# A decoder block on one core: the second FFN's first weights loaded a chunk per gate, the first branch's output and the residual loaded ahead into slots, the mixer's stores on GpSimd's queue

## The chip, the core and the metric

The kernel runs on one core of a Trainium2 chip. The core has TensorE (PE, matrix products into PSUM), VectorE (DVE), ScalarE (ACT), GpSimd (POOL) and SyncE (SP). SP computes nothing here: it issues transfers (DMAs), in the order of its queue, and waits where a transfer's buffer or data isn't ready. GpSimd issues transfers too, also in order, among its few computations. Sixteen DMA engines move the data. The metric is the time of one execution on the device in microseconds (us); lower is better.

## The reference

One layer of a decoder block over 512 tokens of width 1024, all in float32: an FFN, a token mixer and a second FFN, each with its residual, its norm shifted, scaled and gated by vectors computed from a condition `c`.

```python
mod = (silu(c) @ w_ada + b_ada).reshape(3, 3, D)
h = modulate(x, norm_w[0], mod[0,0], mod[0,1]);  x = x + 0.5 * mod[0,2] * swiglu(h, w13[0], w2[0])
h = modulate(x, norm_w[1], mod[1,0], mod[1,1])
proj = h @ w_in                       # latents of the attention, conv_in, gate_logits
o_attn = causal_mla_attention(...)    # 8 heads, blocks of 128 queries
o_conv = gate_b * causal_conv(gate_c * xv)
y_br = [o_attn, o_conv] @ w_branch    # two branches, 512 -> 1024 each
merged = sum(sigmoid(gate_logits) * y_br)
x = x + mod[1,2] * (merged @ w_out)
h = modulate(x, norm_w[2], mod[2,0], mod[2,1]);  x = x + 0.5 * mod[2,2] * swiglu(h, w13[1], w2[1])
```

## The kernel before

All activations lie transposed: eight row tiles (`KD` = 8) of 128 channels by 512 tokens. A float32 product is made of three matmuls (`mm3`, L133): each operand is split into a high part (a cast on ScalarE, L112) and a low part (a subtraction on VectorE, L113), and high x high, high x low and low x high are summed in PSUM. So every weight goes through three steps: a transfer into a raw tile (`raw_load`, L117), the cast, the subtraction.

The mixer has pools of small buffers that are used in turn: `slot` (11 of 128x512), `slot2` (4), `wr` (4 raw weights), `wh` and `wl` (4 high and low halves). Large ones are 17 `block`s. A load into such a buffer waits on its queue until the last user of that buffer is done, and all behind it on the queue wait too.

The order of the mixer around the change is that of the code and of a scheduler which places the instructions on the engines:

- During the attention, the convolution branch and its gates are worked off in between (`under`, L1075). For each row tile `m` of the 8, `gate(1, m, ...)` (L1000) makes a gate product from `w_cg` (8 k-steps, 24 matmuls) and a branch product from `w_br` (4 k-steps, 12 matmuls); the gated result goes out to DRAM (`ycd`, `keep`, L1043), and each head group's attention output to `oad` (L996).
- After the attention, `oad` is read back as `oa` (L1125). Then `gate(0, m, ...)` does the same for the attention branch, and `merge` (L1129) reads `ycd[m]` back into `yc`, adds it, and splits the sum into `mg`, an operand of the output product `wo`. Units of work are run by `stream` (L374): the load of the next unit is issued before the products of this one. After each unit one sum of the condition's vectors (`ada`) is done on VectorE, with its own weight load of 512 KB.
- `out_rows` makes `wo`, 24 matmuls a row tile for the first five; `Residual.put` (L366) forms the new residual from the product and from `xin` (loaded by `fetch`, L359), stores it to `x2d` and feeds the norm `n2`.
- The first weights of the second FFN, eight chunks of 256 KB (`first_raw`, L486, tiles `wfr`), are all issued before the first gate of this stage runs (`wf1`, L1145).

Buffers in the mixer: the gated products, `yc` and `xin` all share the four `slot2`. Queues: everything is on SP's; only the FFNs store on GpSimd's.

Of the kernel before, what the change touches and what calls it, by code (L numbers as in the profile page):

```python
# [13 lines left out]
ALU = mybir.AluOpType  # L14
AX = mybir.AxisListType

P = 128
T = 512
D = 1024
KD = D // P  # L20
# [21 lines left out]
HALF = T // 2  # L42
# [16 lines left out]
def tile_hybrid_block(ctx, tc, xT, pack0, pack1, pos, ada01, ada, w13f0, w13f1, w13a, w13b, w2, w_c, w_cg, w_uq, w_ukv,  # L59
                      w_br, w_out, out):  # L60
    nc = tc.nc
# [8 lines left out]
    def mm(name):  # L70
        return psum.tile([P, T], F32, tag="mm", name=name, bufs=3)

    def aux(name):
        return psum.tile([P, T], F32, tag="aux", name=name, bufs=5)


    def block(name, dt=F32):
        return act.tile([P, 4 * T], dt, tag="block", name=name, bufs=NBLOCK)

    section = {}  # L80
# [9 lines left out]
    def short(tag, n, name, dt=F32):  # L90
        return section["pool"].tile([P, n], dt, tag=tag, name=name, bufs=BUFS[section["kind"]][tag])

    def slot(name, dt=F32):
        return short("slot", T, name, dt)

    def slot2(name, dt=F32):
        return short("slot2", T, name, dt)

    def wide(name, dt=F32):
        return short("wide", WMAX, name, dt)  # L100
# [3 lines left out]
    def halved(t):  # L104
        return t[:, :T], t[:, T:]

    def cols(pair, c0, n):
        return tuple(t[:, c0 : c0 + n] for t in pair)


    def split_to(hi, lo, src):
        nc.scalar.copy(out=hi, in_=src)  # L112
        nc.vector.tensor_tensor(out=lo, in0=src, in1=hi.bitcast(F32), op=ALU.subtract)  # L113
# [6 lines left out]
    def weights(src, n, name):  # L120

        raw = raw_load(src, n, name)
        parts = []
        for c0 in range(0, n, WSUB):
            m = min(WSUB, n - c0)
            hi = short("wh", WSUB, f"wh_{name}_{c0}", F32R)
            lo = short("wl", WSUB, f"wl_{name}_{c0}", F32R)
            split_to(hi[:, :m], lo[:, :m], raw[:, c0 : c0 + m])
            parts.append((hi, lo))
        return lambda i: cols(parts[i * P // WSUB], i * P % WSUB, P)  # L130


    def mm3(ps, a, b, first, last, parts=False):  # L133
        nc.tensor.matmul(ps, a[0], b[0], start=first, stop=False, skip_group_check=parts)  # L134
        nc.tensor.matmul(ps, a[0], b[1], start=False, stop=False, skip_group_check=parts)  # L135
        nc.tensor.matmul(ps, a[1], b[0], start=False, stop=last, skip_group_check=parts)  # L136
# [41 lines left out]
    def mod_col(v, j, n=1):  # L178
        return mod[:, 8 * v + j : 8 * v + j + n]
# [41 lines left out]
    def ada_load(n):  # L221
        for v, k in ada_todo[:n]:
            if section["kind"] == "mixer":
                raw = raw_load(ada[v - 2, k // 2][:, k % 2], D, f"ada_{v}_{k}")
            elif k % 2 == 0:
                pair = block(f"ada_{v}_{k}")
                nc.sync.dma_start(out=pair.rearrange("p (u c) -> p u c", u=2), in_=ada[v - 2, k // 2])
                raw = pair[:, :D]
            else:
                raw = pair[:, D:]  # L230
            ada_ready.append((v, k, raw))
        del ada_todo[:n]
# [16 lines left out]
    def ada_step(n):  # L249
        for _ in range(min(n, len(ada_ready))):  # L250
            ada_unit(*ada_ready.pop(0))
# [98 lines left out]
    class Residual:  # L350
# [8 lines left out]
        def fetch(self, m):  # L359
            if section["kind"] == "ffn":  # L360
                self.xin[m], self.part[m] = halved(wide(f"xin{self.i}_{m}"))
            else:
                self.xin[m] = slot2(f"xin{self.i}_{m}")
            nc.sync.dma_start(out=self.xin[m], in_=self.prev[m])

        def put(self, m, ps, c0=0, n=T):  # L366
            o = self.x[m][:, c0 : c0 + n]
            nc.vector.scalar_tensor_tensor(out=o, in0=ps, scalar=mod_col(self.v, m), in1=self.xin[m][:, c0 : c0 + n],
                                           op0=ALU.mult, op1=ALU.add)
            (nc.gpsimd if section["kind"] == "ffn" else nc.sync).dma_start(out=self.dst[m][:, c0 : c0 + n], in_=o)  # L370

    def stream(units):  # L374
        w = [units[0][0]()]
        yield
        for i, (_, emit) in enumerate(units):
            if i + 1 < len(units):
                w.append(units[i + 1][0]())
            yield from emit(w[i])  # L380

    def whole(name, src, n, rhs, done, spare=False):


        def emit(w):
            ps = mm(f"p_{name}")
            for k in range(n):
                mm3(ps, w(k), rhs[k], k == 0, k == n - 1)
                if k % 4 == 3:
                    if k == n - 1:  # L390
                        done(ps)
                        if spare:
                            if not ada_ready:
                                ada_load(1)
                            ada_step(1)
                            ada_load(min(1, len(ada_todo) - KD))
                    yield

        return (lambda: weights(src, n * P, name), emit)
# [49 lines left out]
    def drain(steps):  # L449
        for _ in steps:  # L450
            pass
# [34 lines left out]
    def first_raw(i, early):  # L486

        n = FIRST[i] * 2 * P
        per = (4 * T if early else WMAX) // n
        for k in range(KD):  # L490
            if k % per == 0:
                t = block(f"wfr{i}_{k}") if early else wide(f"wfr{i}_{k}")
            raw = t[:, k % per * n : (k % per + 1) * n]
            nc.sync.dma_start(out=raw, in_=(w13f0, w13f1)[i][k])
            yield raw
# [308 lines left out]
    n1 = Norm(1, r1.tiles)  # L804
# [71 lines left out]
    oad = dram.tile([4, P, T], F32, name="oad")  # L876
# [66 lines left out]
    class Bank:  # L943
# [38 lines left out]
        def values(self):  # L982
            b, g = self.b, self.g
            if self.h0 == 0:
                po[0] = aux(f"po{b}_{g}")
            for i in range(self.nh):
                h = self.h0 + i
                for kb in range(b + 1):
                    mm3(po[0][:DV, h * P : (h + 1) * P], cols(vb, kb * T + (4 * g + h) * DV, DV),
                        cols(self.pT, (i * (b + 1) + kb) * P, P), kb == 0, kb == b)  # L990
            if self.h0 + self.nh == 4:
                oe = slot(f"oe{b}_{g}")[:, : 2 * P].rearrange("p (c t) -> p c t", c=2)
                for odd in range(2):
                    nc.scalar.copy(out=oe[odd * DV : (odd + 1) * DV],
                                   in_=po[0][:DV].rearrange("p (c o t) -> p c o t", c=2, o=2)[:, :, odd, :])
                nc.sync.dma_start(out=oad[2 * g : 2 * g + 2].rearrange("c p t -> p c t")[:, :, b * P : (b + 1) * P], in_=oe)  # L996

    po = [None]

    def gate(g, m, rhs, done, spare=False):  # L1000

        y = []

        def tanh(pg):
            y.append(slot2(f"gs{g}_{m}"))
            nc.scalar.activation(out=y[0], in_=pg, func=AF.Tanh, scale=0.5)

        def times(py):
            nc.vector.scalar_tensor_tensor(out=y[0], in0=y[0], scalar=1.0, in1=py, op0=ALU.add, op1=ALU.mult)
            done(m, y[0])  # L1010

        return [whole(f"gate{g}_{m}", w_cg[12 + 8 * g + m], KD, n1.h, tanh, spare),
                whole(f"br{g}_{m}", w_br[m][:, 4 * g * P : 4 * (g + 1) * P], 4, rhs, times, spare)]

    oc_b = block("och", F32R), block("ocl", F32R)
    oc = [cols(oc_b, j * T, T) for j in range(4)]
# [24 lines left out]
    ycd = dram.tile([KD, P, T], F32, name="ycd")  # L1041

    def keep(m, y):  # L1043
        nc.sync.dma_start(out=ycd[m], in_=y)

# [74 lines left out]
    oas = [cols(oa_b, j * T, T) for j in range(4)]  # L1122
# [3 lines left out]
        split_to(*oas[j], oa)  # L1126
    mg = [None] * KD

    def merge(m, y):  # L1129
        yc = slot2(f"yc{m}")  # L1130
        nc.sync.dma_start(out=yc, in_=ycd[m])
        nc.vector.tensor_tensor(out=y, in0=y, in1=yc, op=ALU.add)
        if m % 2 == 0:
            mb.append(block(f"mg{m}", F32R))
        z = (m % 2) * 2 * T
        mg[m] = mb[-1][:, z : z + T], mb[-1][:, z + T : z + 2 * T]
        split_to(*mg[m], y)
# [2 lines left out]
    r2 = Residual(2, x1d, 5, x2d)  # L1140
    r2.room()
    n2 = Norm(2, r2.tiles)
    units = [u for m in range(KD) for u in gate(0, m, oas, merge, True)]
    units += out_rows("wo", lambda m: w_out[m], [(0, KD)], mg, r2, n2, (1, 1, 3), True)
    wf1 = list(first_raw(1, True))  # L1145
    wf1 = iter(wf1)
    drain(stream(units))


# [4 lines left out]
            next(n2.steps, None)  # L1154

    r3 = Residual(3, x2d, 8, out)
    ffn(1, n2, ((0, HALF), (HALF, T)), second_chunk, r3, None, (0, 0), wf1)


# [85 lines left out]
```

## Time and profile before

| | us |
|---|---|
| median of the runs shown (3 runs, 1087.56 to 1100.96) | 1089.38 |
| the profiled execution | 1097.2 |
| its span, from the first to the last instruction | 1095.4 |

| share of the span busy | |
|---|---|
| TensorE, matmuls | 95% |
| VectorE | 71% |
| ScalarE | 47% |
| GpSimd | 12% |

In the span the first FFN runs to about 400 us, the mixer to about 750 us (its gates of the attention branch and `wo` from about 627 us), and then the second FFN. The page and the answers of the trace are tables by stretch, lists of waits and instructions in order of time. "SPq" is SP issuing a transfer. PEclk is the granted clock of TensorE as a share of full speed.

### The profile page before, as it was taken

To read this page: it belongs to the slowest core of one execution; us is meant where nothing else is said; L and a number is where in the kernel's file an instruction comes from. 1 tells how busy PE (TensorE), PEld (TensorE's weight loads), DVE (VectorE), ACT (ScalarE), POOL (GpSimd) and SP (SyncE) were. 2 spreads that over 40 slices of the span, in tenths; PEclk is the share of its full clock that TensorE was granted. 3 is DMA by queue.
4 is the path that set the end of the run, shared out by engine and by line. 5 is a ranking of instruction groups with operands and counts; after the bars stand their busy time and mean duration, and the time that the engine had idled before them with its cause. 6 is when DMAs were issued, how large, how long until landed. Compare 5 with 4: busy or idle time off the path is not lost.

```text
span 1095.4 us, 19960 instructions
## 1 busy us (share of the span) xinstructions
PE 1046.0 (95%) x7870; PEld 982.7 (90%) x7870; DVE 782.3 (71%) x1326; ACT 513.9 (47%) x877; POOL 135.7 (12%) x169
## 2 busy tenths in 40 slices
PE   2999989999999989999999989899999999999997
PEld 1999989999999988888887868688999999999997
DVE  6899389855987577767468677648997488834863
ACT  7964345423554154554334433327764255524530
POOL 0001311013100112110000000001101220022001
PEclk9999999999999989999999999899999999999999
DMA  9766987579945423212245486725866894778352
GB/s 367 249 191 197 267 246 206 193 178 272 238 122 205 152 101 97 83 54 68 78 151 187 131 297 235 242 95 155 211 196 223 231 248 128 210 138 216 99 195 85
DMA packets 82254, 198.08 MB, mean 181 GB/s; under 512 B 9584, under 2 KB 12528, under 8 KB 79088
## 3 DMA queue, kind: packets, MB, share of 16 engines
q1 hardware_dynamic: 66256, 164.30, 44.8%
q0 software_dynamic: 15904, 32.51, 15.3%
q8 instruction: 61, 1.00, 0.4%
q14 instruction: 33, 0.27, 0.1%
HBM read 178.95 MB, written 17.83 MB: 180 GB/s over the span
## 4 chain that ended last, share of the span: by engine, by line
PE 76%; DVE 10%; DMA 7%; issue 3%; ACT 1%; SPq 1%; POOL 1%; POOLq 0%; DVEq 0%; ACTq 0%
PE g L134 6%; PE g L135 6%; PE g L136 6%; PE d L135 6%; PE d L136 6%; PE d L134 6%; PE u L134 5%; PE u L135 5%; PE u L136 5%; DMA sa<-in_w13a_dram 2%; DMA wr_ada<-in_ada_dram 2%; DVE ada_acc L199 2%; PE pf L135 1%; PE pf L136 1%; PE pf L134 1%
## 5 line engine op out<-in xcount | busy, mean ns | idle before, releaser
L135 PE MATMUL d<-a,d_h 128*128 128x256 f32 x616 | 171.4, 278 | 1.6 <-DVE a L113 1.6
L136 PE MATMUL d<-a,d_l 128*128 128x256 f32 x616 | 170.9, 278 | 0.0
L134 PE MATMUL d<-a,d_h 128*128 128x256 f32 x616 | 170.9, 278 | 0.0
L134 PE MATMUL u<-T,w_h 128*128 128x256 f32 x456 | 127.8, 280 | 4.0 <-ACT s L567 4.0
L135 PE MATMUL u<-T,w_h 128*128 128x256 f32 x456 | 127.3, 279 | 0.0
L136 PE MATMUL u<-T,w_l 128*128 128x256 f32 x456 | 127.2, 279 | 0.0
L112 ACT CAST w_h<-sa 128x1024 fp32r<-128x1024 f32 x76 | 79.8, 1050 | 81.7 <-issue 48.5
L135 PEld LDWEIGHTS d<-a,d_h 128*128 128x128 f32 x616 | 115.7, 188 | 2.1 <-DVE a L113 2.1
L136 PEld LDWEIGHTS d<-a,d_l 128*128 128x128 f32 x616 | 116.0, 188 | 0.0
L134 PEld LDWEIGHTS d<-a,d_h 128*128 128x128 f32 x616 | 115.9, 188 | 0.0
L113 DVE TENSOR_TENSOR w_l<-sa,w_h 128x1024 fp32r<-128x1024 f32 x76 | 92.5, 1220 | 20.5 <-ACT w_h L112 10.8
L134 PEld LDWEIGHTS u<-T,w_h 128*128 128x128 f32 x456 | 86.2, 189 | 4.9 <-ACT s L567 4.8
L136 PEld LDWEIGHTS u<-T,w_l 128*128 128x128 f32 x456 | 86.7, 190 | 0.0
L135 PEld LDWEIGHTS u<-T,w_h 128*128 128x128 f32 x456 | 86.1, 189 | 0.0
L134 PE MATMUL g<-h,w_h 128*128 128x256 f32 x304 | 84.6, 278 | 0.0
L135 PE MATMUL g<-h,w_h 128*128 128x256 f32 x304 | 84.4, 278 | 0.0
L136 PE MATMUL g<-h,w_l 128*128 128x256 f32 x304 | 84.4, 278 | 0.0
L112 ACT CAST d_h<-wdd 128x1024 fp32r<-128x1024 f32 (+1 forms) x42 | 41.0, 978 | 57.6 <-issue 31.3
L547 DVE TENSOR_TENSOR sb<-sa 128x512 f32<-128x512 f32 x38 | 26.0, 684 | 53.7 <-DMA sa<-in_w13a_dram 32.6
L113 DVE TENSOR_TENSOR d_l<-wdd,d_h 128x1024 fp32r<-128x1024 f32 (+1 forms) x42 | 47.7, 1135 | 16.8 <-ACT d_h L112 11.2
L113 DVE TENSOR_TENSOR w_l<-sb,w_h 128x1024 fp32r<-128x1024 f32 x38 | 46.4, 1220 | 17.5 <-PE g L136 13.5
L136 PEld LDWEIGHTS g<-h,w_l 128*128 128x128 f32 x304 | 57.4, 189 | 0.0
(362 smaller groups left out, 3131.6 us busy)
## 6 DMA issues: line engine op xcount, KB each, us to landing
ada<-in_ada_dram SPq DMA_DIRECT2D x24, 1024.0 KB, 6.7
sa<-in_w13b_dram SPq DMA_DIRECT2D x80, 256.0 KB, 5.0
sa<-in_w13a_dram SPq DMA_DIRECT2D x72, 256.0 KB, 5.3
wdd<-in_w_dram SPq DMA_DIRECT2D x32, 512.0 KB, 4.7
wr_ada<-in_ada_dram SPq DMA_DIRECT2D x24, 512.0 KB, 5.1
sa<-in_w13b_dram POOLq DMA_DIRECT2D x40, 256.0 KB, 6.1
sa<-in_w13a_dram POOLq DMA_DIRECT2D x36, 256.0 KB, 6.3
yd<-yd POOLq DMA_DIRECT2D x32, 256.0 KB, 6.1
```

The lines of the kernel that those rows point to most:

```text
L112: nc.scalar.copy(out=hi, in_=src)
L113: nc.vector.tensor_tensor(out=lo, in0=src, in1=hi.bitcast(F32), op=ALU.subtract)
L134: nc.tensor.matmul(ps, a[0], b[0], start=first, stop=False, skip_group_check=parts)
L135: nc.tensor.matmul(ps, a[0], b[1], start=False, stop=False, skip_group_check=parts)
L136: nc.tensor.matmul(ps, a[1], b[0], start=False, stop=last, skip_group_check=parts)
L199: nc.vector.scalar_tensor_tensor(out=acc, in0=src, scalar=c, in1=acc, op0=ALU.mult, op1=ALU.add)
L547: nc.vector.tensor_tensor(out=b[:, 0], in0=a[:, 3], in1=a[:, 1], op=ALU.add)
```

## The change

- `first_raw` of the second FFN is no longer run through before the stage; each unit that loads branch weights of `gate(0, m, ...)` then calls `ahead(m)`, which loads `ycd[m]` into a `slot` and issues the next chunk of `wfr`.
- `merge` adds the tile that was loaded there and issues no load.
- `xin` of the mixer's residual is a `slot` instead of a `slot2`.
- The stores to `oad`, `ycd` and `x2d` are issued by GpSimd instead of SP.

```diff
@@ Residual.fetch, Residual.put
-                self.xin[m] = slot2(f"xin{self.i}_{m}")
+                self.xin[m] = slot(f"xin{self.i}_{m}")
...
-            (nc.gpsimd if section["kind"] == "ffn" else nc.sync).dma_start(out=self.dst[m][:, c0 : c0 + n], in_=o)
+            nc.gpsimd.dma_start(out=self.dst[m][:, c0 : c0 + n], in_=o)
@@ Bank.values
-                nc.sync.dma_start(out=oad[2 * g : 2 * g + 2].rearrange("c p t -> p c t")[:, :, b * P : (b + 1) * P], in_=oe)
+                nc.gpsimd.dma_start(out=oad[2 * g : 2 * g + 2].rearrange("c p t -> p c t")[:, :, b * P : (b + 1) * P], in_=oe)
@@ gate
-    def gate(g, m, rhs, done, spare=False):
+    def gate(g, m, rhs, done, spare=False, ahead=lambda m: None):
...
-        return [whole(f"gate{g}_{m}", w_cg[12 + 8 * g + m], KD, n1.h, tanh, spare),
-                whole(f"br{g}_{m}", w_br[m][:, 4 * g * P : 4 * (g + 1) * P], 4, rhs, times, spare)]
+        load, emit = whole(f"br{g}_{m}", w_br[m][:, 4 * g * P : 4 * (g + 1) * P], 4, rhs, times, spare)
+
+        def load_ahead():
+            w = load()
+            ahead(m)
+            return w
+
+        return [whole(f"gate{g}_{m}", w_cg[12 + 8 * g + m], KD, n1.h, tanh, spare), (load_ahead, emit)]
@@ keep
-        nc.sync.dma_start(out=ycd[m], in_=y)
+        nc.gpsimd.dma_start(out=ycd[m], in_=y)
@@ merge and the stage's units
+    yc = {}
+
+    def ahead(m):
+        yc[m] = slot(f"yc{m}")
+        nc.sync.dma_start(out=yc[m], in_=ycd[m])
+        wf1.append(next(wf1_loads))
+
     def merge(m, y):
-        yc = slot2(f"yc{m}")
-        nc.sync.dma_start(out=yc, in_=ycd[m])
-        nc.vector.tensor_tensor(out=y, in0=y, in1=yc, op=ALU.add)
+        nc.vector.tensor_tensor(out=y, in0=y, in1=yc[m], op=ALU.add)
...
-    units = [u for m in range(KD) for u in gate(0, m, oas, merge, True)]
+
+    wf1, wf1_loads = [], first_raw(1, True)
+    units = [u for m in range(KD) for u in gate(0, m, oas, merge, True, ahead)]
     units += out_rows("wo", lambda m: w_out[m], [(0, KD)], mg, r2, n2, (1, 1, 3), True)
-    wf1 = list(first_raw(1, True))
-    wf1 = iter(wf1)
     drain(stream(units))
...
-    ffn(1, n2, ((0, HALF), (HALF, T)), second_chunk, r3, None, (0, 0), wf1)
+    ffn(1, n2, ((0, HALF), (HALF, T)), second_chunk, r3, None, (0, 0), iter(wf1))
```

The order of the transfers is where the change is seen. On SP's queue at the start of the attention branch's gates stood, from the read-back `oa` to the branch weights of gate 2 (numbers behind names are the program's buffers):

```order
L1125 DMA oa_7155<-oad 128x512
L1125 DMA oa_7159<-oad 128x512
L494 DMA wfr_0_7165<-in_w13f_dram 128x512 x4
L494 DMA wfr_4_7170<-in_w13f_dram 128x512 x4
L1131 DMA yc_7248<-ycd 128x512
L117 DMA wr_ada_3_7293<-in_ada_dram 128x1024
L117 DMA wr_gate_2_7295<-in_w_cg_dram 128x1024
L1131 DMA yc_7319<-ycd 128x512
L117 DMA wr_ada_4_7326<-in_ada_dram 128x1024
L117 DMA wr_br_2_7328<-in_w_br_dram 128x512
```

and in the changed kernel, at the same place:

```order
L1131 DMA oa_7155<-oad 128x512
L1131 DMA oa_7159<-oad 128x512
L1139 DMA yc_7181<-ycd 128x512
L494 DMA wfr_0_7183<-in_w13f_dram 128x512
L1139 DMA yc_7256<-ycd 128x512
L494 DMA wfr_0_7183<-in_w13f_dram 128x512
L117 DMA wr_ada_3_7288<-in_ada_dram 128x1024
L117 DMA wr_gate_2_7290<-in_w_cg_dram 128x1024
L117 DMA wr_ada_4_7319<-in_ada_dram 128x1024
L117 DMA wr_br_2_7321<-in_w_br_dram 128x512
L1139 DMA yc_7327<-ycd 128x512
L494 DMA wfr_0_7183<-in_w13f_dram 128x512
```

Two chunks of `wfr` now stand ahead of gate 2's weights instead of eight; the others follow, one behind each `yc`.

At the end of the gates SP's queue had, from gate 7's branch weights to the load of the last `yc`:

```order
L117 DMA wr_br_7_7697<-in_w_br_dram 128x512
L117 DMA wr_ada_7_7732<-in_ada_dram 128x1024
L117 DMA wr_wo_0_0_7736<-in_w_out_dram 128x1024
L117 DMA wr_wo_0_0_7784<-in_w_out_dram 128x1024
L1131 DMA yc_7687<-ycd 128x512
L117 DMA wr_wo_0_0_7827<-in_w_out_dram 128x1024
L117 DMA wr_wo_0_0_7869<-in_w_out_dram 128x1024
L117 DMA wr_wo_0_0_7911<-in_w_out_dram 128x1024
L364 DMA xin_0_7734<-x1d 128x512
L1131 DMA yc_7760<-ycd 128x512
```

and has now:

```order
L117 DMA wr_br_7_7696<-in_w_br_dram 128x512
L1139 DMA yc_7702<-ycd 128x512
L494 DMA wfr_4_7486<-in_w13f_dram 128x512
L117 DMA wr_ada_7_7734<-in_ada_dram 128x1024
L364 DMA xin_0_7736<-x1d 128x512
L117 DMA wr_wo_0_0_7738<-in_w_out_dram 128x1024
L364 DMA xin_1_7782<-x1d 128x512
L117 DMA wr_wo_0_0_7784<-in_w_out_dram 128x1024
L117 DMA wr_wo_0_0_7827<-in_w_out_dram 128x1024
```

The last `yc` stood behind five loads of `wo` weights and now stands behind gate 7's branch weights, ahead of all of them. On GpSimd's queue, which had nothing between the attention's powers and the norm's, stand now the stores; these are its rows from the last of the attention to the second FFN:

```order
L996 DMA oad<-oe_0_6942 128x2x128
L1050 DMA ycd<-gs_7_7034 128x512
L996 DMA oad<-oe_1_7141 128x2x128
L370 DMA x2d<-x_0_7163 128x512 x4
L370 DMA x2d<-x_1_7164 128x512
L370 DMA x2d<-x_1_7164 128x256 x3
L287 TENSOR_TENSOR nr_0_8098<-nv_0_8096,mhalf 128x2
L370 DMA x2d<-x_1_7164 128x256 x3
L287 TENSOR_TENSOR nr_2_8275<-nv_2_8273,mhalf 128x2
L537 DMA sa_2_8469<-in_w13b_dram 128x512
```

The computations on GpSimd keep their order; the stores are put between them. On TensorE the order of the matmuls is the same but for a few around the first two branch k-steps.

## Rows read from the trace of the kernel before

**Rows 1.** Page, part 1: busy us (share of the span) xinstructions.

```profile
PE 1046.0 (95%) x7870; PEld 982.7 (90%) x7870; DVE 782.3 (71%) x1326; ACT 513.9 (47%) x877; POOL 135.7 (12%) x169
```

**Rows 2.** By stretches: length; busy PE, PEld, DVE, ACT, POOL; PEclk, DMA share, GB/s.

```profile
630.00:640.00 10.00, 9.43 (x40) 6.97 (x38) 5.16 (x9) 2.57 (x5) 0.00 (x0) 1.00 1.01 378
670.00:680.00 10.00, 10.00 (x44) 8.03 (x43) 6.90 (x12) 2.87 (x5) 0.00 (x0) 1.00 0.79 277
700.00:710.00 10.00, 6.33 (x15) 4.67 (x16) 5.84 (x10) 3.33 (x5) 0.00 (x0) 0.66 0.60 179
900.00:1000.00 100.00, 100.00 (x884) 100.00 (x884) 61.98 (x83) 46.35 (x65) 14.76 (x18) 1.00 0.66 155
```

**Rows 3.** Waits of TensorE, 440 to 780 us: total us, times, longest.

```profile
PE wo L134 <- ACT mg L112: 3.4, 1, 3.4
PE p_gate L134 <- ACT wh_gate L112: 2.6, 1, 2.6
...
PE wo L135 <- DVE mg L113: 0.4, 1, 0.4
PE p_br L134 <- ACT oah L112: 0.3, 1, 0.3
```

**Rows 4.** TensorE in order of time: start, us, form [idle before <- releaser].

```profile
642.30 0.50 PE L134 MATMUL p_gate<-h,wh_gate 128*128 128x512 f32 x1 [2.58 <-ACT wh_gate L112]
...
677.21 0.39 PE L134 MATMUL p_gate<-h,wh_gate 128*128 128x512 f32 x1
...
699.55 0.40 PE L136 MATMUL wo<-mg,wl_wo 128*128 128x512 f32 x1
703.32 0.79 PE L134 MATMUL wo<-mg,wh_wo 128*128 128x512 f32 x1 [3.37 <-ACT mg L112]
...
709.33 0.50 PE L134 MATMUL wo<-mg,wh_wo 128*128 128x512 f32 x1
```

**Rows 5.** ScalarE in order of time, the same columns.

```profile
630.14 0.62 ACT L112 CAST oah<-oa 128x512 fp32r<-128x512 f32 x1
...
641.63 1.14 ACT L112 CAST wh_gate<-wr_gate 128x512 fp32r<-128x512 f32 x2 [2.56 <-DMA wr_gate<-in_w_cg_dram]
```

**Rows 6.** SP's queue in order of time: start, us, transfers issued.

```profile
624.40 0.37 SPq L996 DMA_DIRECT2D oad<-oe  x1
...
626.71 0.94 SPq L1125 DMA_DIRECT2D oa<-oad  x2
627.70 4.13 SPq L494 DMA_DIRECT2D wfr<-in_w13f_dram  x8
...
633.69 0.33 SPq L117 DMA_DIRECT2D wr_gate<-in_w_cg_dram  x1
...
689.37 6.27 SPq L117 DMA_DIRECT2D wr_wo<-in_w_out_dram  x3
...
696.16 0.42 SPq L1131 DMA_DIRECT2D yc<-ycd  x1
```

**Rows 7.** VectorE in order of time, columns as in rows 4.

```profile
676.52 0.69 DVE L113 TENSOR_TENSOR wl_gate<-wr_gate,wh_gate 128x512 fp32r<-128x512 f32 x1 [1.34 <-ACT wh_gate L112]
...
692.61 0.69 DVE L1132 TENSOR_TENSOR gs<-gs,yc 128x512 f32<-128x512 f32 x1 [0.60 <-DMA yc<-ycd]
...
695.80 0.68 DVE L1009 SCALAR_TENSOR_TENSOR gs<-gs,p_br 128x512 f32<-128x512 f32 x1
...
701.92 0.69 DVE L1132 TENSOR_TENSOR gs<-gs,yc 128x512 f32<-128x512 f32 x1 [4.84 <-DMA yc<-ycd]
...
703.73 0.68 DVE L113 TENSOR_TENSOR mg<-gs,mg 128x512 fp32r<-128x512 f32 x1
```

**Rows 8.** Tiles `x1d`, `x2d`: issues (ns min/median/max), landing of `x1d`, of `x2d` (also loads).

```profile
L370 POOL DMA_DIRECT2D x1d<-x x12: 539/540/584, 351.6 to 391.6; - x12
...
DMA to landing us min/median/max: 2.0/2.8/5.9
DMA to landing us min/median/max: 1.7/2.6/4.9
```

## The prediction

> **What bounds the kernel now.** I read the page first: TensorE is busy 95% of the span [rows 1], so only the stretches in which it is not busy, or runs slowly, can give time back. The table by stretches places them for the stage that is changed: 900 to 1000 us, the second FFN, has TensorE busy for all 100 us, while 700 to 710 us has 6.33 us of 10 and a granted clock of 0.66 [rows 2]. Then the list of waits of TensorE from 440 to 780 us, mixer and start of the second FFN: the two largest are 3.4 us for an operand of the output product `wo` (a cast to `mg`), plus 0.4 us for its low part, and 2.6 us for gate weights [rows 3]. They are what the change can reach, as the next three views show.
>
> The first stall ends at 642.30 us: a matmul of gate 2 waits 2.58 us [rows 4]. What it waits for is the cast of the gate's weights on ScalarE at 641.63 us, and that stood idle 2.56 us for the transfer [rows 5]. The transfer was issued at 633.69 us, behind eight `wfr` loads that take SP's queue from 627.70 us for 4.13 us [rows 6]. They are 8 x 256 KB = 2.1 MB, and with all else 630 to 640 us moved 378 GB/s at a DMA share of 1.01 [rows 2]: 2.1 MB at that rate are 5.5 us. So this stall is the eight loads' doing.
>
> The second stall ends at 703.32 us, after 3.37 us [rows 4], and the low part adds 0.4 us [rows 3]. It is row tile 7 of the merged branches. VectorE has its gated product at 695.80 us, then stands 4.84 us until `yc` lands and adds it at 701.92 us; the low part follows at 703.73 us [rows 7]. That `yc` load was issued only at 696.16 us, behind three `wr_wo` loads which hold SP's queue from 689.37 us for 6.27 us [rows 6]. What it reads was stored by the stage before, so it is late only by its place in the queue and its wait for a `slot2`.
>
> This stall has a second price. From 699.55 us (the last matmul before it) to 709.33 us (the first that comes at the old pace again) there are 13 steps [rows 4]. The matmuls around it start every 0.233 us; those between start every 0.427 us, in the stretch whose granted clock is 0.66 [rows 2]: the lower of the two levels, 1.2 instead of 2.4 GHz. 13 steps at 0.233 us are 3.03 us; they took 9.78 us. The stall thus costs 6.75 us: some 3.75 us of waiting and 3 us of slow clock. The first stall has no such tail.
>
> **The change, part by part.**
>
> *First weights a chunk per gate.* The same eight loads, the same bytes, now one behind each `yc` load. Ahead of gate 2's weights stand two instead of eight: 1.5 MB fewer, at 378 GB/s 4.2 us, and six issues fewer, of 4.13/8 = 0.52 us each. The gate's transfer would be issued near 631 us and land near 636 to 638 us, where it was 641.6 us; TensorE wants it at 642.30 - 2.58 = 639.72 us. Gain 2.58 us. Ahead of it on VectorE now stand two sums of `ada` and one low part, about 0.7 us each, which end before 640 us if the transfers land by 637.5 us. If the bandwidth is what 670 to 680 us shows, 277 GB/s [rows 2], they land a little later and half a microsecond comes back; I count that below.
>
> The six other chunks go into the gates 2 to 7. There the weights have one raw buffer per gate, so each load waits until VectorE has split the one before, and the slack is small: for gate 6 the first low half is done at 676.52 + 0.69 = 677.21 us [rows 7] and TensorE starts at 677.21 us, needing it from its third matmul on, 0.47 us later [rows 4]. If TensorE comes 2.58 us earlier, the weights must as well. They start earlier by about as much, since the whole ring hangs on gate 2's split. But a chunk of 256 KB takes 0.9 us at 277 GB/s, and it stands ahead of the `ada` and gate loads of its turn. Lower bound nothing (the queue is idle for microseconds between a branch's load and the next), upper bound 0.9 us in each of six gates, 5.4 us. I take 0.5 us: one late gate, since the bound is reached only if nothing of the chunk moves in the idle time, and the DMA share in 670 to 680 us is 0.79.
>
> *The first branch's output loaded ahead.* Same eight loads, each now issued right behind the branch weights of its own gate. Those weights must be there before the branch product starts, 12 matmuls or 2.8 us before the product is done, and `yc` lands soon after them: no wait for it is left. After the change the add comes as soon as VectorE has done the product and the reduction that stands between (0.6 us each); from the start of the add to the end of the low part the rows have 703.73 - 701.92 + 0.68 = 2.49 us. So the low part is ready near 695.80 + 0.6 + 0.6 + 2.5 = 699.5 us, counted on the old times. Also gone is the wait of the tile before it, 0.60 us on the same engine [rows 7]. TensorE would ask for it at 699.78 us at the earliest. That is close, but everything ahead of it shifts with the first stall. Gain 6.75 us, lower bound 3 us (a wait of 1 us left and some slow clock), upper bound 6.75 us.
>
> *The residual in slots.* `xin` leaves the four `slot2` buffers for eleven slots. No wait of TensorE after 709 us names it, so nothing is gained; its cover is the 5.6 us that each row of `wo` takes. Loads 2 to 7 now stand behind `wr_wo` loads; VectorE needs load 2 only after three rows of products. Nothing, unless that cover is gone, and then as late as the load.
>
> *Stores on GpSimd's queue.* Twenty-seven stores leave SP's queue: eight `oad`, eight `ycd`, eleven `x2d`. SP waited for their data, but the list names no wait of TensorE for weights before gate 2's, so nothing is gained there. GpSimd issues one in 0.54 us (`x1d` in the first FFN, twelve of the shapes of `x2d`) [rows 8]. What queues behind them there is the norm's power (`nr`), wanted microseconds after the last store, and that of the attention; both keep their cover. One store is on the path: the last `oad`, issued at 624.40 us, is read back by two loads at 626.71 us [rows 6], and their cast at 630.14 us [rows 5] makes TensorE wait 0.3 us already [rows 3]. From GpSimd the store takes 0.2 us more to issue (0.54 against 0.37 us), and landing goes by the medians 2.8 against 2.6 us for stores of `x` on the two queues; the worst are 5.9 and 4.9 us [rows 8]. So 0.4 us lost, bounds 0 and 3.5 us (5.9 against the 2.3 us that this one took).
>
> The Trainium skill (SBUF — State Buffer, section "SBUF: two separate sides") says that a DMA issued from GpSimd has its descriptors written by that engine, which VectorE locks out while it runs in certain modes; it gives 620 ns alone against 3100 ns beside such a copy. By it the last store would be 2.5 us late and the gain smaller by as much. The rows of `x1d`, 539 to 584 ns beside a busy VectorE, don't show it.
>
> **Sum.** 2.58 + 6.75 - 0.5 - 0.4 = 8.4 us. The profiled execution took 1097.2 us, so it would take 1088.8 us; it lies 7.8 us above the median of the runs shown, 1089.4 us. If the stalls are the same there, the median becomes **1081.0 us**. The second FFN is bound by TensorE, so it starts and ends earlier by all of it.
>
> **The rivals.**
>
> *The gate ring gives the first stall back.* For it: the 0.47 us of slack and a DMA share that rises from 0.79 to about 0.9 (0.9 us of transfer in the 36 matmuls or 8.4 us of a gate). Against: the ring starts earlier too. Only the second stall is gained, with the store's 0.4 us and up to 2 us more lost: 1089.4 - 6.35 = 1083.0 us, up to 1085 us.
>
> *The store is late on GpSimd.* 2.5 to 3.5 us at the first branch product instead of 0.4 us: 1083.1 to 1084.1 us. A lock by VectorE would do it (the page above); the rows speak against it.
>
> *The operand stays late.* The last `mg` waits for its turn on VectorE behind splits of `wo` weights that themselves land late. Half or all of the 6.75 us stays: 1084.4 to 1087.7 us. For it: the weights' transfers and the add share one engine in order. Against: the product was there at 695.80 us.
>
> *Slower: the chunks starve the ring.* `yc` and chunk, 512 KB a gate, stand ahead of `ada` and gate weights, 1.8 us at 277 GB/s; six gates late by that are 10.9 us, and one stall as long as the second brings the slow clock, 3.0 us more. Against the gain of 9.3 us this is a loss of 4.6 us: 1094 us. It decides from 1.55 us of delay per gate on. Against: the bytes are the same in all and far fewer before 640 us, and a transfer that stands ahead of another costs it nothing when it goes out microseconds earlier.
>
> **Chances.** Forecast 0.62, the ring gives back 0.13, store late 0.08, operand late 0.10, slower 0.07. 1076 to 1090 us: below it 1080 less the scatter of some 3 us about the lowest of the runs shown; above it the slower case. About 2% is what a measurement of this kernel can tell from no change; that is 22 us, and all stalls within reach add up to 9.6 us. So faster by over 2% 0.01, within 2% 0.97, slower by over 2% 0.02 (the ring late by 4 us a gate).
>
> **What would show it.** Gate 2 without a wait, and 630 to 640 us with a DMA share under 0.9: the first step. No wait of `wo` for `mg`, and a granted clock of 1.00 through the stretch of `wo`: the second. The wait of the first branch product for `oah` of 0.5 to 0.9 us: the store. A new wait at gates 5 or 6 is the ring. It is wrong if TensorE's idle time in 600 to 710 us doesn't fall, or if the second FFN takes longer.

## The result and the profile after

The changed kernel takes 1084.42 us (median of 20 runs, 1082.0 to 1096.28) where the kernel before, timed beside it, takes 1093.12 us (20 runs, 1086.19 to 1105.61). The ratio is 0.9933, 95% interval [0.9912, 0.9955]: 7.3 us less, between 4.9 and 9.6. That is no change by the 2% bound, and a small gain that the interval keeps away from 1. The profiled execution took 1083.25 us, its span 1081.4 us.

Page of the changed kernel, part 1, to set beside [rows 1]: busy us (share) xinstructions.

```profile
PE 1037.5 (96%) x7870; PEld 976.3 (90%) x7870; DVE 782.1 (72%) x1326; ACT 514.2 (48%) x877; POOL 151.9 (14%) x196
```

The work is the same; GpSimd alone has more of it, 196 instructions instead of 169, which are the 27 stores. The waits of TensorE from 440 to 780 us, as in [rows 3], now name neither `wh_gate` nor `mg`:

```profile
PE pf L136 <- DVE wfl L113: 1.2, 2, 0.7
...
PE p_br L134 <- ACT oah L112: 0.4, 1, 0.4
```

Stretches of the changed kernel, columns as in [rows 2]:

```profile
630.00:640.00 10.00, 10.00 (x45) 8.05 (x44) 8.78 (x14) 3.26 (x6) 0.00 (x0) 1.00 0.97 347
700.00:710.00 10.00, 10.00 (x44) 8.02 (x43) 4.48 (x7) 2.66 (x5) 1.08 (x2) 1.00 0.56 212
900.00:1000.00 100.00, 100.00 (x885) 100.00 (x884) 60.10 (x80) 45.71 (x64) 18.25 (x21) 1.00 0.72 179
```

700 to 710 us had TensorE busy for 6.33 us at a granted clock of 0.66; now it is busy throughout at 1.00, and 630 to 640 us too. The second FFN runs as before (885 matmuls in 100 us against 884).

The next two views give the reasons. SP's queue of the changed kernel, columns as in [rows 6]:

```profile
624.50 0.36 SPq L1139 DMA_DIRECT2D yc<-ycd  x1
624.90 0.43 SPq L494 DMA_DIRECT2D wfr<-in_w13f_dram  x1
...
626.86 0.38 SPq L117 DMA_DIRECT2D wr_gate<-in_w_cg_dram  x1
...
672.20 0.42 SPq L1139 DMA_DIRECT2D yc<-ycd  x1
```

and its VectorE, columns as in [rows 7]:

```profile
687.92 0.68 DVE L1009 SCALAR_TENSOR_TENSOR gs<-gs,p_br 128x512 f32<-128x512 f32 x1
...
689.12 0.69 DVE L1143 TENSOR_TENSOR gs<-gs,yc 128x512 f32<-128x512 f32 x1
...
690.91 0.69 DVE L113 TENSOR_TENSOR mg<-gs,mg 128x512 fp32r<-128x512 f32 x1
```

Gate 2's weights are issued at 626.86 us behind two chunks (before: 633.69 us, behind eight [rows 6]). The last `yc` is issued at 672.20 us, 15.7 us ahead of the product it is added to (before: 696.16 us, behind that product [rows 6, 7]). Its add has no idle time ahead of it, and the last low part of `mg` starts 2.99 us after its product instead of 7.93 us.

**The yardstick.** Executions of one and the same kernel lie up to 20 us apart (last section), so the variants below are told apart by two parts of the stage, read from TensorE's timeline of each profile: from the first product of the attention branch (`p_br<-oah`) to the first of `wo`, which holds the first stall, and from there to the first sum of the norm behind `wo` (`ps_ss`), which holds the second. The three matmuls in before:

```profile
627.69 0.39 PE L134 MATMUL p_br<-oah,wh_br 128*128 128x512 f32 x1
...
694.80 0.48 PE L134 MATMUL wo<-mg,wh_wo 128*128 128x512 f32 x1
...
740.10 0.58 PE L282 MATMUL ps_ss<-ones_c,nacc 128*128 128x1 f32 x4
```

and in after:

```profile
624.31 0.39 PE L134 MATMUL p_br<-oah,wh_br 128*128 128x512 f32 x1
...
688.23 0.48 PE L134 MATMUL wo<-mg,wh_wo 128*128 128x512 f32 x1
...
726.68 0.58 PE L282 MATMUL ps_ss<-ones_c,nacc 128*128 128x1 f32 x4
```

| kernel | branch to `wo`, us | `wo` to norm sum, us | both |
|---|---|---|---|
| before | 67.11 | 45.30 | 112.41 |
| after | 63.92 | 38.45 | 102.37 |
| after once more (e11) | 64.28 | 38.45 | 102.73 |

The stage is 10.0 us shorter. The spans of the profiled pair differ by 14.0 us; of the rest, 3.4 us lie ahead of the stage (it starts at 627.7 and at 624.3 us, and over all kernels here anywhere from 622.5 to 627.7 us, whatever the edit), and 0.6 us behind it.

### The profile page after: what moved, and what is told of

Its sections match the earlier page's. It is cut to its first block, busy times and chain, and to the rows that moved or that the text cites. A ratio compares the mean times of both kernels' runs of the same rounds, so it can differ in the third digit from the quotient of the medians.

```text
span 1081.4 us, 19989 instructions
## 1 busy us (share of the span) xinstructions
PE 1037.5 (96%) x7870; PEld 976.3 (90%) x7870; DVE 782.1 (72%) x1326; ACT 514.2 (48%) x877; POOL 151.9 (14%) x196
## 4 chain that ended last, share of the span: by engine, by line
PE 58%; issue 14%; DVE 3%; POOL 2%; DMA 1%; ACT 1%; POOLq 0%; DVEq 0%; ACTq 0%; SPq 0%
PE d L135 5%; PE d L136 5%; PE d L134 5%; PE g L134 4%; PE g L135 4%; PE g L136 4%; PE u L134 3%; PE u L135 3%; PE u L136 3%; PE p_gate L136 2%; PE p_gate L134 2%; PE p_gate L135 2%; PE wo L134 1%; PE wo L135 1%; PE wo L136 1%
## 5 line engine op out<-in xcount | busy, mean ns | idle before, releaser
L134 PEld LDWEIGHTS g<-h,w_h 128*128 128x128 f32 x304 | 57.2, 188 | 0.2 <-ACT s L572 0.2
```

## The experiments

**One part undone at a time.** First the chunks, all eight up front again (e1):

```diff
-    wf1, wf1_loads = [], first_raw(1, True)
-        wf1.append(next(wf1_loads))      # in ahead(m)
+    wf1 = list(first_raw(1, True))       # before the units run
```

> The changed kernel, but the eight chunks of the second FFN's first weights are all issued ahead of the stage again. Theory A (each stall has its own cause, the chunks the first): TensorE waits 2 to 3 us for gate 2's weights, no wait for the last mg; from the first gate of the stage to wo 73.5 us instead of the changed kernel's 70.5 us, from wo to the second half's norm sum 38.5 us as in the changed kernel; 3 us above the changed kernel. Rival B (the loads ahead and the stores, not the chunks, free gate 2): no wait at gate 2, the changed kernel's time.

Measured: 69.47 and 38.45 us; time 1096.18 us, ratio to before 0.9967 [0.9929, 1.0005]. The first stall is back, alone and larger: waits of TensorE from 440 to 780 us in this kernel,

```profile
PE p_gate L134 <- ACT wh_gate L112: 3.7, 1, 3.7
```

and its stretches (columns as in [rows 2]):

```profile
640.00:650.00 10.00, 7.80 (x26) 5.93 (x27) 7.63 (x12) 3.10 (x6) 0.00 (x0) 0.83 0.74 232
...
850.00:900.00 50.00, 50.00 (x427) 50.00 (x426) 30.14 (x42) 19.46 (x28) 12.68 (x17) 1.00 0.89 238
```

Two loads of `yc` now stand ahead of gate 2's weights, where before had one, which fits a wait of 3.73 us instead of 2.58 us; and here it is followed by half speed: granted clock 0.83, seven steps of about 0.427 us between matmuls. The price is 69.47 - 63.92 = 5.6 us. Theory A has the cause right, and both of its sizes (2 to 3 us of wait, 3 us in all) are too small. The chunks per gate are what removes the first stall, and with `yc` loaded ahead they are worth 5.6 us instead of the 67.11 - 63.67 = 3.4 us that they bring alone (e4 below). The row of 850 to 900 us is taken up in the last section.

Then `yc` in the merge again, from a `slot2` (e2):

```diff
-        yc[m] = slot(f"yc{m}")                     # in ahead(m)
-        nc.sync.dma_start(out=yc[m], in_=ycd[m])
+        yc = slot2(f"yc{m}")                       # in merge
+        nc.sync.dma_start(out=yc, in_=ycd[m])
```

> The changed kernel, but yc is loaded in merge from slot2 again, the chunks stay one per gate. Theory A: no wait at gate 2; the wait of wo for the last mg is back, 3 to 4 us, and with it a granted clock near 0.66 in the ten us after, so 45 us instead of 38.5 us from wo to the norm sum; 6 to 7 us above the changed kernel. Rival B (xin in its own slots is what frees the last yc, since xin and yc no longer share slot2): no wait, the changed kernel's time.

Measured: 64.75 and 39.21 us; 1095.67 us, ratio 0.9973 [0.9935, 1.0011]. The second stall does not come back; of the waits for `mg` only this one is left:

```profile
PE wo L135 <- DVE mg L113: 0.5, 1, 0.5
```

This was the miss that mattered: with `yc` late in the code, and still in a `slot2`, it lands in time but for 0.5 us. So something else of the change must also remove the second stall.

Then the three stores on SP's queue again (e3):

```diff
-            nc.gpsimd.dma_start(out=self.dst[m][:, c0 : c0 + n], in_=o)   # so also oad, ycd
+            (nc.gpsimd if section["kind"] == "ffn" else nc.sync).dma_start(out=self.dst[m][:, c0 : c0 + n], in_=o)
```

> The changed kernel, but the stores to oad, ycd and x2d stay on SP's queue. Theory A (the stores cost and bring nothing): the changed kernel's time within 1 us, the wait for oah 0.3 instead of 0.4 us, no wait at gate 2 or at the last mg. Rival B (the stores hold SP's queue and so the loads behind them): waits of TensorE for gate weights or for mg of more than 1 us, 2 to 6 us above the changed kernel.

Measured: 63.89 and 38.46 us, as in after to 0.03 us; 1093.44 us, ratio 0.9962 [0.9925, 0.9999]. Between these two kernels the stores neither gain nor cost anything that the stage shows: the wait for `oah` is 0.25 us here and 0.40 us in after, and the part is no shorter. Two other pairs of kernels are set beside this one further down.

**One part alone.** The kernel before with the chunks per gate and nothing else (e4):

> The kernel before, with only the chunks of first weights spread, one per gate. Theory A: the wait at gate 2 is gone, the wait for the last mg stays at 3 to 4 us with its slow clock: 3 us under the kernel before. Rival B (the ring of gate weights gives the gain back): waits of 2 us or more at gates 5 to 7, the time of the kernel before.

Measured: 63.67 and 44.54 us; 1097.52 us, ratio 1.0008 [0.9976, 1.0039]. The first stall is gone, the second is whole (waits of TensorE, 440 to 780 us):

```profile
PE wo L134 <- ACT mg L112: 3.4, 1, 3.4
...
PE wo L135 <- DVE mg L113: 0.7, 1, 0.7
```

What holds the last `yc` stands in the chain of waits of the kernel before, which the prediction did not read (start, us, what the chain passes through):

```profile
686.81 0.61 DVE wl_gate L113
...
687.44 0.33 SPq L117
...
687.82 4.69 DMA yc<-ycd
...
692.61 0.70 DVE gs L1132
...
694.59 0.69 DVE wl_wo L113
...
695.31 0.33 SPq L117
...
695.68 0.42 SPq L364
...
696.16 5.66 DMA yc<-ycd
```

Read from the top: a gate's low half frees a raw buffer, only then SP can issue a `wr_wo` (L117), and `yc` 6 goes out behind it and lands at 692.5 us. VectorE, in order, adds it at 692.61 us and so comes to the split of a `wo` weight only at 694.59 us; that frees the raw buffer for the next `wr_wo` at 695.31 us; behind it on SP's queue stands `xin` 0 (L364), and behind that `yc` 7. One late load makes the next one late, through VectorE and the raw buffers, and `xin` 0 is a link, though by itself it holds the queue only from 695.68 to 696.16 us, 0.48 us. `yc` 7 does not wait for its `slot2`: it goes out as soon as `xin` 0 is issued.

The next run (e5) tests that: the kernel before, with the chunks per gate and the residual in slots; `yc` and stores as before.

```diff
-                self.xin[m] = slot2(f"xin{self.i}_{m}")
+                self.xin[m] = slot(f"xin{self.i}_{m}")
```

> The kernel with yc late, but the stores on SP's queue: chunks per gate and xin in slots are all that is left of the change. Theory A (the slots of xin are what lets the last yc go out earlier, since xin 0 no longer stands between): at most 1 us of waits for the last mg, granted clock 1.00 through wo, 38.5 to 39.5 us from wo to the norm sum. Rival B (the stores on SP held it): a wait of 3 us or more for mg, some 45 us.

Measured: 64.02 and 38.69 us, 1084.01 us in a single execution (before, a single one: 1101.61 us). Both stalls are gone without `yc` ahead. It differs from e4 in the residual's buffers alone, and the second part falls from 44.54 to 38.69 us (39.74 in e10, the same kernel): with the chunks per gate, the residual in slots is enough. SP's queue of this kernel:

```profile
679.01 0.33 SPq L117 DMA_DIRECT2D wr_wo<-in_w_out_dram  x1
679.40 0.41 SPq L1140 DMA_DIRECT2D yc<-ycd  x1
679.91 6.86 SPq L117 DMA_DIRECT2D wr_wo<-in_w_out_dram  x4
686.83 0.43 SPq L1140 DMA_DIRECT2D yc<-ycd  x1
```

`yc` 6 stands behind one `wr_wo`, and no `xin` stands ahead of `yc` 7: that one goes out 2.03 us before the first matmul of `wo` (688.86 us), where before it went out 1.36 us after it (696.16 against 694.80 us). The 0.48 us of `xin` 0 are a small part of that. The order of the queue has changed too: in before and e4 two `wr_wo` loads stand ahead of `yc` 6. What it does is seen in VectorE's add of `yc` 6, in e4

```profile
689.32 0.69 DVE L1141 TENSOR_TENSOR gs<-gs,yc 128x512 f32<-128x512 f32 x1 [0.92 <-DMA yc<-ycd]
```

and in e5:

```profile
683.76 0.68 DVE L1141 TENSOR_TENSOR gs<-gs,yc 128x512 f32<-128x512 f32 x1
```

In e4 VectorE still waits 0.92 us for `yc` 6 (0.60 us in before [rows 7]), in e5 not at all: there the chain no longer runs through `yc` 6.

The kernel before with only `yc` loaded ahead (e6):

> The kernel before with yc loaded ahead into slots, and nothing else: chunks up front, xin in slot2, stores on SP. Theory A (each stall has its own cause): 2.5 to 4 us of wait at gate 2, none for mg, 38.5 us from wo to the norm sum. Rival B (the second stall is a late consequence of the first, through the ring of gate weights): the wait for mg stays at 1 us or more.

Measured: 70.07 and 38.45 us; 1089.04 us in a single execution. The second stall is gone, with `xin` left in `slot2`. The first has grown as in e1 (3.22 us, granted clock 0.96 and 0.87 in 630 to 650 us); the part costs 70.07 - 67.11 = 3.0 us more than before. And with only the stores on GpSimd (e7):

> The kernel before with the stores to oad, ycd and x2d on GpSimd's queue, and nothing else. Theory A: both stalls stay, 2.5 us or more at gate 2 and 3 us or more for mg with the slow clock, about 67 us to wo and 45 us on to the norm sum. Rival B (without stores on SP's queue the loads of gate 2 and of the last yc go out in time): one of the two waits falls under 1 us.

Measured: 67.71 and 44.61 us; 1095.33 us in a single execution. Both stalls stay: 3.0 us at gate 2, 2.5 and 0.4 us at `wo`, granted clock 0.66 in 700 to 710 us.

**The residual alone, and the two edits timed.** Timed side by side: before with only `xin` in slots (e9), the kernel of e5 again (e10), and the changed kernel again (e11).

> The kernel before with one edit: the residual `xin` in the eleven slots instead of the four `slot2` buffers; the eight `wfr` loads stay up front, `yc` stays in the merge and in `slot2`, the stores stay on SP's queue. Theory A (a chain: the second stall needs `xin` 0 ahead of `yc` 7 on SP's queue and in `slot2`): this alone removes it, wait of `wo` for `mg` at most 1 us, 38.4 to 39.5 us from the first matmul of `wo` to the first norm sum (44.5 to 45.3 with the stall, 38.45 without), gate 2's wait stays at 2.5 to 3.7 us, 67 to 68 us from the first branch product to `wo`. Theory B (the prediction's step: `xin` brings nothing, `yc` is late by its own place behind the `wr_wo` loads): the wait of 3 us or more stays, 44 to 46 us. Theory C (the chunks per gate are needed too, since in the run of chunks and `xin` slots both were there): 41 us or more, and the wait between 1 and 3 us.

Measured: 68.31 and 41.01 us; 1095.97 us, ratio 0.9986 [0.9941, 1.0031]. Its waits of TensorE, 440 to 780 us:

```profile
PE p_gate L134 <- ACT wh_gate L112: 2.1, 1, 2.1
PE wo L134 <- ACT mg L112: 1.4, 1, 1.4
...
PE wo L135 <- DVE mg L113: 0.7, 1, 0.7
PE p_gate L136 <- DVE wl_gate L113: 0.6, 1, 0.6
```

Neither theory A (38.4 to 39.5 us) nor B (44 to 46 us) holds by its numbers; theory C does, at its edge (41 us or more, 1 to 3 us of wait). This edit takes 45.30 - 41.01 = 4.3 of the 6.85 us: the slow clock (granted clock 1.00 in 700 to 710 us) and 1.7 us of the wait. The rest needs the chunks per gate or `yc` ahead. What in the chunks brings it was not tried; SP's queue shows only that `yc` 6 stands here behind two `wr_wo` loads, as in before, where in e5 it stood behind one:

```profile
681.90 0.93 SPq L117 DMA_DIRECT2D wr_wo<-in_w_out_dram  x2
682.88 0.42 SPq L1131 DMA_DIRECT2D yc<-ycd  x1
684.43 6.25 SPq L117 DMA_DIRECT2D wr_wo<-in_w_out_dram  x3
690.74 0.43 SPq L1131 DMA_DIRECT2D yc<-ycd  x1
```

VectorE waits 0.60 us for `yc` 6 here as in before, so the chain is still there, only earlier. Against the first matmul of `wo`, `yc` 7 goes out 1.46 us sooner than in before: 0.48 us are `xin` 0, the other 1.0 us the `wr_wo` load ahead of it. Why that load is sooner is not shown. The stall at gate 2 costs 68.31 - 67.11 = 1.2 us more here, and loads that do not wait for TensorE may have got ahead by it; so the 4.3 us are not for certain the residual's alone. The comparison of e4 and e5 has no such doubt, since neither has a stall at gate 2.

> The kernel before with the chunks one per gate and `xin` in slots, no more; seen once before with 64.02 and 38.69 us in the stage's two parts (after: 63.92 and 38.45). Theory A: these two edits are the whole gain, so its time and that of the changed kernel in this same call differ by less than 0.3%, and its ratio to the kernel before is 0.990 to 0.997. Theory B: the loads of `yc` ahead or the stores on GpSimd bring something that the stage's two parts don't show: then it is slower than the changed kernel by 0.3% or more.

Measured: 64.18 and 39.74 us (0.65 us of wait for a low part of `mg`); 1091.22 us, ratio 0.9957 [0.9911, 1.0003].

> The changed kernel once more, on the chip of this call. By the stage: 63.9 us from the first branch product to `wo` and 38.5 us to the first norm sum, 10 us less than the kernel before, whatever the pace of the FFNs. By the time: a ratio of 0.990 to 0.995 if the stage is all there is; 0.996 or more if the FFNs give part of it back.

Measured: 64.28 and 38.45 us; 1086.07 us, ratio 0.9917 [0.9869, 0.9966], before 1094.22 us. By the stage the two kernels differ by 1.2 us, by the medians by 5.15 us, 0.5%. Both kernels' times fall into two groups with 5.5 us or more between them (e10: five runs from 1083.74 to 1087.55 and five from 1094.90 to 1098.84; e11: eight from 1080.53 to 1089.83 and two above 1095), so the medians depend on how many fell into each, and ten runs don't settle it. By the medians theory A fails (under 0.3%) and theory B's 0.3% is reached, but the scatter is larger than either. Whether `yc` ahead is worth more than the stage's 0.3 to 1.2 us over these two edits stays open.

**The second stall over all kernels.** The issue of the last `yc` against the first matmul of `wo`, from the two timelines:

| kernel | last `yc` issued, us from the first `wo` matmul | waits of `wo` for `mg`, us | `wo` to norm sum, us |
|---|---|---|---|
| e4, chunks only | +1.65 | 3.4 + 0.7 | 44.54 |
| before | +1.36 | 3.4 + 0.4 | 45.30 |
| e7, stores only | +1.14 | 2.5 + 0.4 | 44.61 |
| e9, `xin` only | -0.10 | 1.4 + 0.7 | 41.01 |
| e10, chunks and `xin` | -0.44 | 0.65 | 39.74 |
| e2, all but `yc` ahead | -1.12 | 0.5 | 39.21 |
| e5, chunks and `xin` | -2.03 | none | 38.69 |
| after | -16.03 | none | 38.45 |

The three at the top lie within 0.8 us and are not in order; below them the part gets shorter the sooner `yc` goes out. Of the kernels not listed, e1, e3, e6 and e11 have it out 17 to 33 us ahead and take 38.45 or 38.46 us, and e8 (below) has it out 13 us ahead, its 39.44 us holding a wait for a `wo` weight. With `yc` out 1.12 us ahead 0.5 us of wait was left, with 2.03 us none; the change has it out 16 us ahead.

**The ring loaded harder.** The rival "slower" said that more bytes ahead of the gates' weights starve them. The changed kernel with 512 KB more per gate (e8), in two loads into slots that nothing reads:

```diff
         wf1.append(next(wf1_loads))
+        for z in range(2):
+            nc.sync.dma_start(out=slot(f"more{m}_{z}"), in_=ycd[m])
```

> The changed kernel with 512 KB more per gate: two more loads of 256 KB behind each chunk, into slots that nobody reads. Theory A (the ring of gate weights has some slack; a chunk of 256 KB fits, three times as much does not): waits of 0.5 to 2 us at several of the gates 3 to 7, in all 3 to 8 us more from the first branch product to wo. Rival B (the queue's idle time takes them): no wait at a gate, 64 us to wo as in the changed kernel. Rival C of the prediction (the chunks already fill the ring): 10 us or more.

Measured: 68.20 and 39.44 us; 1092.40 us in a single execution. Its waits of TensorE, 440 to 780 us:

```profile
PE p_gate L136 <- DVE wl_gate L113: 2.2, 2, 1.2
...
PE p_gate L134 <- ACT wh_gate L112: 0.8, 1, 0.8
PE wo L136 <- DVE wl_wo L113: 0.7, 1, 0.7
```

768 KB a gate instead of 256 KB cost 68.20 - 63.92 = 4.3 us, with waits at gates 2 and 6 (theory A had the sum, not the gates): the rival's mechanism exists at three times the chunk. What lies between was not tried. How much of it is bandwidth (630 to 640 us: 387 GB/s) and how much the waits for two more slots, this run does not part.

## Why the prediction was right, step by step

The forecast was a gain of 8.4 us and no change by 2%. Measured are 7.3 us [4.9, 9.6] and, timed a second time, 1094.22 x 0.0083 = 9.1 us [3.7, 14.3] by the ratios, and 10.0 and 9.7 us in the stage of the profiles. Right in class and near in size; not every step was right. That 8.4 lies so near 7.3 us is partly luck: for the stage the sum is 1.6 us short (3.2 + 6.85 = 10.0 us against 8.4), by 0.6 us of the first stall, 0.1 of the second, 0.5 of the ring and 0.4 of the stores.

- **First stall, 2.58 us.** Right in its cause: e1 and e4 show that the eight chunks made it and the chunks per gate remove it. The size was too small: the part fell by 67.11 - 63.92 = 3.2 us. The prediction took the listed wait alone and wrote that this stall has no tail. It has a short one, in before:

```profile
639.32 0.40 PE L136 MATMUL p_br<-oah,wl_br 128*128 128x512 f32 x1
...
643.44 0.40 PE L134 MATMUL p_gate<-h,wh_gate 128*128 128x512 f32 x1
```

  Between these two lie four steps; they took 4.12 us, where four at 0.233 us are 0.93 us: 3.19 us.
- **The ring, 0.5 us lost.** No loss is seen: no gate waits, and the kernels with chunks per gate (after, e2 to e5, e10, e11) lie between 63.67 and 64.75 us. e8 shows how far the limit is.
- **Second stall, 6.75 us.** The size was right, half speed included: 45.30 - 38.45 = 6.85 us. The timing too: low part ready 690.91 + 0.69 - 687.92 = 3.7 us after the start of the product, predicted 699.5 - 695.8 = 3.7 us.
- **"Late only by its place in the queue and its wait for a `slot2`"; "the residual in slots: nothing is gained".** This is the step that failed. In e2 `yc` keeps its place in the code, behind five `wr_wo` loads, and its `slot2`, and comes in time; between e4 and e5 the residual alone is worth 4.8 to 5.9 us, between before and e9 4.3 us. The stall was held by a chain over SP's queue, VectorE and the raw buffers, which more than one edit breaks. The prediction saw the `wr_wo` loads ahead of `yc` 7 but not what the last of them waited for, and it asked only whether TensorE waits for `xin`, not what stands behind `xin`'s load. The sum was right because it counted the stall once, and it needs removing only once: e6 (`yc` alone) and e5 (`xin` and chunks) both reach it, so the two edits do not add up.
- **Stores on GpSimd, 0.4 us lost.** Neither shown nor refuted. Three pairs of kernels differ in the stores alone. From SP to GpSimd the wait for `oah` goes from 0.25 us (e3) to 0.40 and 0.35 (after, e11), from 0.29 (before) to 0.62 (e7), and from 0.37 and 0.52 (e5, e10) to 0.79 (e2); the part goes from 63.89 us to 63.92 and 64.28, from 67.11 to 67.71, and from 64.02 and 64.18 to 64.75. So the part is 0.0 to 0.7 us longer, where two profiles of one kernel lie up to 0.36 us apart. Tile `oad`, of after:

```profile
L996 POOL DMA_DIRECT2D oad<-oe x8: 713/723/766, 453.0 to 621.3; - x8
...
DMA to landing us min/median/max: 2.2/3.2/4.9
```

and of e3, stores on SP:

```profile
L996 SPq DMA_DIRECT2D oad<-oe x8: 370/380/427, 452.3 to 620.8; - x8
...
DMA to landing us min/median/max: 1.8/3.2/5.2
```

  That is 0.34 us more to issue (the prediction took 0.2 us, from a store of another shape) and the same median landing; the rival's 2.5 us is seen nowhere. The Trainium skill (SBUF — State Buffer, section "SBUF: two separate sides") says that VectorE locks GpSimd out of writing descriptors while it runs in certain modes. The rows show no delay of that size: 766 ns at most, where by its 3100 ns, an estimate, the last store would have been over 2 us late. No trace here shows whether VectorE ran in such a mode beside these stores, so the rule is not tested.
- **A marker that was wrong.** 630 to 640 us should have had a DMA share under 0.9; it has 0.97. The queue is nearly as full as before (347 against 378 GB/s), but gate 2's weights left it first: the order made the wait, not the load.
- **The level, 1081.0 us.** The median is 3.4 us above it, because the kernel before has 1093.12 us over 20 runs and not the 1089.38 us of three.
- **Rivals.** "The ring gives it back" and "the store is late" by 2.5 us or more did not come, as shown above. "The operand stays late" did not come (no wait for `mg`), though its link, splits of `wo` weights on VectorE that land late, is part of the real chain. "Slower" needs more than 256 KB of chunk a gate.

Beyond the two stalls: the stage says 10 us, the first ratio 7.3 us with 10 outside its interval. Whether all executions of before have both stalls in the size of the profiled one is not known, and the pace below moves the times by as much; that difference stays open. The ratios alone would not have told the variants apart: e1 and e3 have 0.9967 and 0.9962, though their stages differ by 5.6 us, and e3 has the stage of after, whose ratio is 0.9933. By the stage, no variant here beats the changed kernel.

## What to carry to other kernels

When an operand is late, follow its load back through the queue until something is reached that isn't itself waiting: each load, buffer and in-order engine on that way is a place where an edit can help, here one was enough (e6), and edits that break the same chain do not add up. An edit is not worth nothing because no engine waits for its own data; ask also what is queued behind it. And where executions scatter by more than the change is worth, compare the distance between two fixed instructions in the profiles.

## What the hardware showed that was not expected

**Two paces at one granted clock.** The FFNs' streams of 128x256 matmuls run at one of two spacings, with TensorE busy throughout and a granted clock of 1.00 in both. From 850 to 900 us, before has

```profile
850.00:900.00 50.00, 50.00 (x444) 50.00 (x443) 30.18 (x42) 21.05 (x30) 12.13 (x17) 1.00 0.92 244
```

and e1 (above) 427 matmuls, e3 428. One execution can have both, as e4 has:

```profile
870.00:920.00 50.00, 50.00 (x444) 50.00 (x443) 41.13 (x60) 26.63 (x38) 9.21 (x11) 1.00 0.80 209
950.00:1000.00 50.00, 50.00 (x427) 50.00 (x426) 17.87 (x20) 16.10 (x22) 11.14 (x14) 1.00 0.66 147
```

In the timelines the matmuls start 113.3 or 117.8 ns apart; the mixer's 512-column matmuls kept 230 to 234 ns in all kernels. From the norm sum to the end, e1, e2 and e3 take 364.8 to 366.3 us, before, after, e5 to e7 and e9 to e11 354.2 to 355.9 us, e8 357.6 and e4 360.0 us: that is the order of the scatter in the times. The DMA share does not part the two (0.92 and 0.89 above), nor does any edit. What sets the pace is open. The four kernels timed together on one chip, e1 to e4, all have the slower spacing at least in part, and the kernel before, timed beside them, has a median of 1099.07 us, against 1093.12 and 1094.22 us in the other two series; so the chip or the moment may set it, which no run here tests.

**The price of a stall is not its length.** At gate 2, 2.58 us of waiting in before and 3.0 us in e7 kept a granted clock of 1.00, while 2.1 + 0.6 us in e9 brought 0.93 and 0.90 in 630 to 650 us, and 3.73 us in e1 brought 0.83. At `wo`, 2.5 + 0.4 us in e7 brought 0.66, and 1.4 + 0.7 us in e9 brought nothing. About the same wait cost 3.2 us in before and 68.31 - 63.92 = 4.4 us in e9, both measured against the part without a stall.
